# Attention on head pairs: scores on row halves and values on column halves of TensorE, denominators summed on VectorE and GpSimd

## The chip, the cores and the metric

The kernel runs on all eight cores of one Trainium2 chip, each core on two of the 16 sequences. The metric is device time in microseconds of the slowest core. Some executions fall in a slow state, in which the cores of one die show a lower granted TensorE clock. Single cores also ran at a clock of 0.98 in runs that count as fast. Where that matters I quote the median span of the *undisturbed cores*: all cores, over all runs of a kernel, with a granted clock of at least 0.984.

## The reference

One layer of an encoder: half-step SwiGLU FFN, then a mixer with two head groups, then a second FFN. The change touches the forgetting attention in the mixer (8 heads of 64):

```python
def fox_attention(q, k, v, log_f):                 # (B,S,H,64), causal
    F = cumsum(log_f)                              # decay, per head
    s = q·k * 64**-0.5 + F[t] - F[s]               # keys s <= t
    p = softmax(s)
    return p @ v
```

Width 1024, sequence 2048, FFN width 2816, two sequences per core. The kernel works on eight groups of 512 tokens per core, four per sequence. A group's mixer looks at 4, 8, 12 or 16 key tiles of 128.

## The kernel before

Each operation is recorded with what it reads and writes. A list scheduler with a price for every operation then fixes one static order per engine: mixer work has priority on TensorE, and FFN work of other token groups fills the rest. Attention went head by head, on the full 128 x 128 array. The queries of one head were padded with 64 rows of zeros, and each head's values stood beside 64 columns of ones, so that the second half of the output was the softmax denominator:

```python
V = sb("V", [128, 4, 16, 192], BF16)      # [v of even head | ones | v of odd head]
QT = sb("QT", [128, 8, T], BF16)          # one head per slot, the other 64 rows are zero
mixw = sb("mixw_t", [128, 2, 2048], BF16)
Pt = hM                                   # probabilities live in the tile of normalised inputs
...
for h in range(8):
    p, odd = h // 2, h % 2
    ob = 6 + nxt("ob", 2)
    def pv(j, r, off, W):
        lhsT = V[:, p, j, 64:192] if odd else V[:, p, j, 0:128]
        MM(banks[ob][:, off:512], [(lhsT, Pt[:, r, 0:W])], ...)
    for j in range(nj):                   # key tiles
        MM(banks[b][:, 0:W], [(KT[:, p, j * 128:(j + 1) * 128], QT[:, h, off:512])], ...)
        ACTV([... AF.Exp ...])            # ScalarE, 256 columns at a time
        if jj >= 0:
            TT(Pt[:, r, 0:128], Pt[:, r, 0:128], mask01[:], ALU.mult, ..., eng="pool")
        ...                               # pv follows two tiles later
    for q in range(4):                    # 64-row reciprocals, then one multiply
        P.op("dve", lambda e, ...: e.reciprocal(out=o_, in_=i_), ...)
    TT(cc[drow, p, :], banks[ob][drow, :], rcp[drow, :], ALU.mult, ...)
```

The FFN was scheduled in pieces of 8 matmuls (gate, up) and 11 (down).

## Time and profile before

| | before |
|---|---|
| first six runs | median 2773.08 us (2769.96 to 3190.63; the two high ones are slow) |
| profiled run, slowest core | 2773.5 us |
| TensorE busy | 2652.1 us, 96% |
| VectorE, ScalarE, GpSimd busy | 1487.3, 971.4, 260.2 us |

From the page of the kernel before, its span, part 1 (busy time and share of the span by engine, instructions) and the first line of part 4 (the chain of work that ended last):

```profile
span 2773.5 us, 42864 instructions; the slowest of 8 cores (2765.4 to 2773.5 us)
PE 2652.1 (96%) x14704; PEld 1294.4 (47%) x14704; DVE 1487.3 (54%) x2340; ACT 971.4 (35%) x2065; POOL 260.2 (9%) x479
...
PE 83%; DMA 7%; DVE 7%; issue 3%; ACT 1%; POOL 0%; DVEq 0%; POOLq 0%; SPq 0%; ACTq 0%
```

TensorE bounds the kernel. Its busy time is not its work, though. The timeline of the kernel before shows it (columns: start, duration, engine, line, operation, out<-in, form as rows*columns of the array):

```profile
1214.08 0.38 PE L310 MATMUL bank<-hM,V 128*128 128x512 bf16 x1
1214.29 0.38 PE L310 MATMUL bank<-QT,KT 128*128 128x512 bf16 x1
1214.51 0.38 PE L310 MATMUL bank<-hM,V 128*128 128x512 bf16 x1
```

Each matmul is recorded as 0.38 us, but one starts every 0.2155 us, so the records overlap. Scores and values alternate without a gap. So I count *slots*. A slot is the start-to-start time of a matmul's width: the median in this trace is 0.216 us for 512 columns, 0.163 for 384, 0.109 for 256, 0.056 for 128, and about 0.027 for the smallest. This is the formula N/2.4 + 2.5 ns of the Trainium skill, "TensorE: Matmul & The Clock Gate", Back-to-back issue gap. The section calls it the gap of isolated matmuls and gives about 131 ns (512 columns) and 81 ns (128) for a sustained stream; in this trace the stream itself has the formula's 216 and 56 ns, so I use the formula to fill a table of slots.

The groups that the change touches, kernel before (count, then busy us and mean ns, then idle time before them):

```profile
L310 PE MATMUL bank<-hM,V 128*128 128x512 bf16 x448 | 165.8, 380 | 10.6 <-DVE cc L347 6.1 <-POOL hM L347 4.3 <-issue 0.2
L310 PE MATMUL bank<-QT,KT 128*128 128x512 bf16 x448 | 157.1, 379 | 0.0
...
L347 POOL TENSOR_TENSOR hM<-hM,mask 128x128 bf16<-128x128 bf16 x256 | 109.3, 436 | 473.7 <-ACT hM L335 473.2 <-issue 0.2
```

And what TensorE waited for, kernel before (total us, times, longest):

```profile
PE bank L310 <- ACT sqF L335: 17.8, 12, 9.3
PE bank L310 <- DMA wgu<-wgus: 15.0, 6, 5.4
PE bank L310 <- DVE cc L347: 13.2, 12, 6.2
...
PE bank L310 <- DMA mixw_t<-mixws: 5.8, 6, 1.9
```

### The profile page before, as it was taken

How to read it: one execution, taken by the hardware profiler on the slowest of the kernel's cores; microseconds unless marked ns; L12 is line 12 of the kernel's file. 1: busy time of each engine (PE TensorE's matmuls, PEld its weight loads, DVE VectorE, ACT ScalarE, POOL GpSimd, SP SyncE). 2: the span in 40 equal slices, each digit the busy share in tenths (PEclk: the TensorE clock that was granted, in tenths of full speed). 3: DMA queues.
4: the chain of work that ended last, by engine and by line, in shares of the span. 5: the costliest groups of instructions: out<-in, count | busy, mean ns of one | idle time of the engine just before them, and what ended most of it. 6: DMA issues, size and time to landing. Idle time of an engine off the chain costs nothing.

```text
span 2773.5 us, 42864 instructions; the slowest of 8 cores (2765.4 to 2773.5 us)
## 1 busy us (share of the span) xinstructions
PE 2652.1 (96%) x14704; PEld 1294.4 (47%) x14704; DVE 1487.3 (54%) x2340; ACT 971.4 (35%) x2065; POOL 260.2 (9%) x479
## 2 busy tenths in 40 slices
PE   5999998899999999999999999999999999999997
PEld 2444453444454444544445444554445444544433
DVE  4334558458556535555455844567345575565433
ACT  2112313325327314177131421345112563375111
POOL 1100002022011000001000210011000110010000
PEclk9999999999999999999999999999999999999999
DMA  7866665587775644424444364433644334443453
GB/s 176 188 150 149 166 193 127 130 165 147 214 193 130 191 152 137 141 95 138 156 141 141 113 204 152 137 124 107 197 143 146 111 95 138 133 118 101 151 156 112
DMA packets 123585, 406.08 MB, mean 146 GB/s; under 512 B 14303, under 2 KB 14448, under 8 KB 122608
## 3 DMA queue, kind: packets, MB, share of 16 engines
q1 hardware_dynamic: 102688, 329.32, 36.9%
q0 software_dynamic: 20256, 73.24, 14.8%
q8 instruction: 125, 2.05, 0.3%
q10 hardware_dynamic: 432, 0.79, 0.1%
q14 instruction: 84, 0.69, 0.1%
HBM read 395.25 MB, written 59.77 MB: 164 GB/s over the span
## 4 chain that ended last, share of the span: by engine, by line
PE 83%; DMA 7%; DVE 7%; issue 3%; ACT 1%; POOL 0%; DVEq 0%; POOLq 0%; SPq 0%; ACTq 0%
PE bank L310 83%; DVE hM L780 2%; DMA wgu<-wgus 2%; DMA wgu<-wgu 1%; DMA mixw_t<-mixws 1%; DVE hF L350 1%; DVE x_sb L350 1%; DVE hM L350 1%; DVE thF L350 1%; DMA mixw_t<-mixw 1%; DMA wd<-wd 1%; DVE cc L347 0%; DVE act L347 0%; DMA y<-x_sb 0%; DMA x_sb<-x 0%
## 5 line engine op out<-in xcount | busy, mean ns | idle before, releaser
L310 PE MATMUL bank<-hF,wgu 128*128 128x512 bf16 x5280 | 1212.7, 382 | 37.6 <-DMA wgu<-wgus 15.0
L310 PEld LDWEIGHTS bank<-hF,wgu 128*128 128x128 bf16 x5280 | 508.9, 98 | 640.9 <-issue 69.9
L310 PE MATMUL bank<-act,wd 128*128 128x512 bf16 x2640 | 600.2, 379 | 4.8 <-DMA wd<-wd 3.3
L335 ACT ACTIVATE thF<-bank 128x512 f32<-128x512 f32 x352 | 210.6, 598 | 985.5 <-PE bank L310 984.6
L335 ACT ACTIVATE hM<-bank,biasT 128x256 bf16<-128x256 f32 (+1 forms) x1152 | 437.9, 471 | 144.4 <-PE bank L310 143.1
L350 DVE SCALAR_TENSOR_TENSOR thF<-thF,bank 128x512 f32<-128x512 f32 x352 | 241.4, 686 | 459.7 <-ACT thF L335 457.7
L310 PEld LDWEIGHTS bank<-act,wd 128*128 128x128 bf16 x2640 | 248.5, 98 | 287.7 <-issue 9.8
L350 DVE SCALAR_TENSOR_TENSOR x_sb<-bank,x_sb 128x512 f32<-128x512 f32 x256 | 176.7, 690 | 292.8 <-PE bank L310 291.0
L347 DVE TENSOR_TENSOR act<-bank,thF 128x512 bf16<-128x512 f32 x330 | 227.4, 689 | 170.4 <-PE bank L310 167.5
L780 DVE RECIPROCAL hM<-bank 64x128 f32<-64x128 f32 x256 | 244.4, 955 | 51.9 <-PE bank L310 36.1
L310 PE MATMUL bank<-hM,V 128*128 128x512 bf16 (+3 forms) x640 | 196.0, 348 | 10.8 <-DVE cc L347 6.1
L310 PE MATMUL bank<-hM,mixw_t 128*128 128x512 bf16 x896 | 199.8, 379 | 2.9 <-DMA mixw_t<-mixws 2.7
L310 PE MATMUL bank<-QT,KT 128*128 128x512 bf16 (+3 forms) x640 | 202.4, 347 | 0.0
L335 ACT ACTIVATE sqF<-x_sb 128x512 bf16<-128x512 f32 x176 | 108.3, 627 | 222.2 <-DVE x_sb L350 179.2
L347 POOL TENSOR_TENSOR hM<-hM,mask 128x128 bf16<-128x128 bf16 x256 | 109.3, 436 | 473.7 <-ACT hM L335 473.2
L310 PE MATMUL bank<-mixw_t,hM 128*128 128x256 bf16 x1280 | 143.8, 273 | 6.1 <-DMA mixw_t<-mixws 3.1
L310 PEld LDWEIGHTS bank<-mixw_t,hM 128*128 128x128 bf16 x1280 | 124.8, 98 | 27.1 <-issue 8.8
L310 PEld LDWEIGHTS bank<-hM,mixw_t 128*128 128x128 bf16 x896 | 86.4, 98 | 107.9 <-issue 8.1
L310 PE MATMUL bank<-cc,mixw_t 128*128 128x512 bf16 x512 | 121.2, 388 | 9.3 <-DVE cc L347 7.1
L434 POOL TENSOR_TENSOR stpM<-stvM,mhalf 128x8 f32<-128x8 f32 (+1 forms) x26 | 36.6, 1407 | 672.1 <-DVE stvM L354 672.0
L310 PEld LDWEIGHTS bank<-hM,V 128*128 128x128 bf16 x640 | 60.7, 98 | 76.8 <-issue 17.1
L434 POOL TENSOR_TENSOR stpF<-stvF,mhalf 128x4 f32<-128x4 f32 x22 | 23.5, 1069 | 708.9 <-DVE stvF L354 708.9
(114 smaller groups left out, 1545.2 us busy)
## 6 DMA issues: line engine op xcount, KB each, us to landing
wgu<-wgus SPq DMA_DIRECT2D x275, 512.0 KB, 3.8
wd<-wds SPq DMA_DIRECT2D x200, 352.0 KB, 3.2
mixw_t<-mixws SPq DMA_DIRECT2D x112, 512.0 KB, 3.9
wgu<-wgu POOLq DMA_DIRECT2D x55, 512.0 KB, 6.4
wgus<-wgu SPq DMA_DIRECT2D x44, 512.0 KB, 5.6
wd<-wd POOLq DMA_DIRECT2D x40, 352.0 KB, 5.8
wds<-wd SPq DMA_DIRECT2D x32, 352.0 KB, 4.0
x_sb<-x POOLq DMA_DIRECT2D x5, 2048.0 KB, 11.1
```

The costliest lines, as they stand in the source:

```text
L310: ins = e.matmul(out, lhsT=l, rhs=r, start=s0, stop=s1)
L335: ins = e.activation(out=out, in_=in_, func=func, **kw)
L347: return DVE(lambda e: e.tensor_tensor(out=out, in0=a, in1=b, op=op), free_n(out), reads, writes, rate, eng, level)
L350: return DVE(lambda e: e.scalar_tensor_tensor(out=out, in0=a, scalar=s, in1=b, op0=op0, op1=op1), free_n(out), reads, writes, level=level)
L434: P.op("pool", lambda e: e.tensor_tensor(out=pw[:, 0:n], in0=v[:, 0:n], in1=mhalf[:, 0:n], op=ALU.pow), [("stv", who), "mhalf"], [("stp", ...
L780: P.op("dve", lambda e, o_=rcp[drow, qs], i_=banks[ob][srow, qs]: e.reciprocal(out=o_, in_=i_), [], [PS(ob), ("hM", 6), ("hM", 7)], dur=86 ...
```

## The change

Its intent is to use both halves of the array in attention. Two heads form a pair. Their scores contract over 64 rows each, in the upper and the lower row half, at the same time. Their values fill 64 columns each, in the two column halves, at the same time. The ones columns go, so the probabilities are added up over the key tiles by VectorE (even head) and GpSimd (odd head), and four matmuls of 512 columns per pair of heads (each head's sum in two bf16 parts) with a 64-column block of ones sum over the partitions. Work comes in groups of two key tiles x two heads: two scores steps, then the values step of the group before, kept together by a new `glue` in the scheduler. (The scheduler's code and the placement of a few projections are left out.)

```diff
-        mixw = sb("mixw_t", [128, 2, 2048], BF16)
+        mixw = sb("mixw_t", [128, 3, 2048], BF16)
-        V = sb("V", [128, 4, 16, 192], BF16)
-        QT = sb("QT", [128, 8, T], BF16)
+        V = sb("V", [128, 4, 16, 128], BF16)
+        Pt = sb("Pt", [128, 8, T], BF16)
+        QT = sb("QT", [128, 4, T], BF16)
...
+        def PAIRS(items, reads, writes, switch=206.0, level=None):
+            d = switch + sum(free_n(items[i][2]) / 2.4 + 9.0 for i in range(0, len(items), 2))
...
-  [(0, 8)]                                        # FFN pieces, gate and up
+  [(0, 4), (4, 8)]
-  [(0, NC2 - 1), (NC2 - 1, NC2)] if d == 0 else [(0, NC2)]      # down
+  (0, 5), (5, NC2 - 1), (NC2 - 1, NC2)
...
+            def scores(p, js):                    # two key tiles, two heads each
+                    for e in range(2):
+                        rows = slice(64 * e, 64 * e + 64)
+                        items.append((banks[bs[2 * q + e]][:, 0:512 - off], KT[rows, p, j * 128:(j + 1) * 128],
+                                      QT[rows, p, off:512], True, True))
...
+            def probabilities(p, tiles):          # Exp on ScalarE, mask now on VectorE, then the sums
+                    for j, e, r, off, b in tiles:
+                        TT(den[:, e, off:512], den[:, e, off:512], Pt[:, r, 0:512 - off], ALU.add, [("Pt", r)], [("ga", e)],
+                           eng=("dve", "pool")[e])
+            def values(p, tiles):
+                for j, e, r, off, b in tiles:
+                    half = slice(64 * e, 64 * e + 64)
+                    items.append((banks[OB][half, off:512], V[:, p, j, half], Pt[:, r, 0:512 - off], j == 0, j == nj - 1))
+            def normalize(p):                     # split the sum into two bf16 parts, ones64 matmuls, reciprocals
...
+            for p in range(4):
+                for j in range(0, nj, 2):
+                    mm, tiles = scores(p, (j, j + 1))
+                    if last is not None:
+                        mm.glue = values(*last)
+                    if last is not None and j == 0:
+                        normalize(last[0])
+                    probabilities(p, tiles)
+                    last = (p, tiles)
```

More of the change, by code (lines that the diff above doesn't have):

```diff
@@ L27 @@
     __slots__ = ("eng", "fn", "reads", "writes", "dma_key", "stream", "idx", "deps", "waits", "signal",
-                 "count", "clock", "gidx", "dur", "lat", "prio", "start", "end", "nbytes", "users", "rate", "tset", "slack")
+                 "count", "clock", "gidx", "dur", "lat", "prio", "start", "end", "nbytes", "users", "rate", "glue", "tset", "slack")
 class Prog:
@@ L40, in op @@
         o.slack = slack
+        o.glue = None
         o.tset = tset
@@ L73, in schedule @@
             o.deps = list(deps.values())
+        for o in reversed(ops):
+            if o.glue is not None:
+                have = {id(d) for d in o.deps}
+                o.deps += [d for d in o.glue.deps if id(d) not in have and d is not o]
+                if o not in o.glue.deps:
+                    o.glue.deps.append(o)
+        for o in ops:
             for d in o.deps:
@@ L86, in schedule @@
         n_done = 0
+        placed = [False] * len(ops)
+        glued = None
         while n_done < len(ops):
@@ L89, in schedule @@
             for e in ENGINES:
+                while ready[e] and placed[ready[e][0][1]]:
+                    heapq.heappop(ready[e])
+                while soon[e] and placed[soon[e][0][1]]:
+                    heapq.heappop(soon[e])
                 if ready[e]:
@@ L97, in schedule @@
                     best = (t, e)
-            t, e = best
-            while soon[e] and soon[e][0][0] <= t:
-                g = heapq.heappop(soon[e])[1]
-                heapq.heappush(ready[e], (ops[g].prio, g))
-            g = heapq.heappop(ready[e])[1]
+            if glued is not None:
+                e, g = glued.eng, glued.gidx
+                t = free[e]
+            else:
+                t, e = best
+                while soon[e] and soon[e][0][0] <= t:
+                    g = heapq.heappop(soon[e])[1]
+                    if not placed[g]:
+                        heapq.heappush(ready[e], (ops[g].prio, g))
+                g = heapq.heappop(ready[e])[1]
             o = ops[g]
+            placed[g] = True
+            glued = o.glue
             o.start = t
@@ L275, in build_nc @@
         mhalf = sb("mhalf", [128, 16], F32)
+        ones64 = sb("ones64", [128, 64], BF16)
+        tick = sb("tick", [128, 1], F32)
         ident = sb("ident", [128, 128], BF16)
@@ L288, in build_nc @@
         wmisc = sb("wmisct", [128, 8, 40], BF16)
-        Pt = hM
-        flat = V[:].rearrange("p a b c -> p (a b c)")
-        hF2 = flat[:, 0:8 * T].rearrange("p (k t) -> p k t", k=8)
-        act2 = flat[:, 8 * T:(8 + NC2) * T].rearrange("p (k t) -> p k t", k=NC2)
+        hF2 = KT[:].rearrange("p a b -> p (a b)")[:, 0:8 * T].rearrange("p (k t) -> p k t", k=8)
+        act2 = V[:].rearrange("p a b c -> p (a b c)")[:, 0:NC2 * T].rearrange("p (k t) -> p k t", k=NC2)
         glT = pieces[96:128, :]
-        rcp = hM[:, 6:8, :].rearrange("p k t -> p (k t)").bitcast(F32)
+        rcp = sqM[:].rearrange("p r t -> p (r t)").bitcast(F32)
+        den = ga[:].rearrange("p (e t) c -> p e (t c)", e=2)
+        den_hi = lsg[:].rearrange("p (e t) c -> p e (t c)", e=2)
+        den_lo = kdec[:].rearrange("p (e t) c -> p e (t c)", e=2)
+        osum = gv[:].rearrange("p (r t) c -> p r (t c)", r=2).bitcast(F32)
         osq = hM[:, 6:8, :]
@@ L321, in MMS @@
             d = sum(max(free_n(r) / 2.4 + 3.0, 27.0) for _, _, r, _, _ in items)
+            return P.op("pe", mm_fn(items), reads, writes, dur=d, lat=280.0, level=level)
+        def PAIRS(items, reads, writes, switch=206.0, level=None):
+            d = switch + sum(free_n(items[i][2]) / 2.4 + 9.0 for i in range(0, len(items), 2))
             return P.op("pe", mm_fn(items), reads, writes, dur=d, lat=280.0, level=level)
@@ L398, in build_nc @@
         MSET(wg2a[96:128, :], 0.0, ["wg2a"], eng="dve")
-        MSET(QT[64:128, 0:8:2, :], 0.0, [("QT", p) for p in range(4)], eng="dve")
-        MSET(QT[0:64, 1:8:2, :], 0.0, [("QT", p) for p in range(4)], eng="dve")
+        MSET(ones64[:], 1.0, ["ones64"])
         MSET(pieces[0:96, :], 0.0, ["pieces"], eng="dve")
@@ L488, in ffn @@
                     bg = nxt("fb", 3)
-                    for k0, k1 in ([(0, 4), (4, 5), (5, 6), (6, 7), (7, 8)] if cnt["wgu"] == 1 else [(0, 8)]):
-                        MM(banks[bg][:], [(w4[:, 0, k, :], L.h[:, k, :]) for k in range(k0, k1)],
-                           [("wgu", wb)] + L.hk[k0:k1], [PS(bg)], start=k0 == 0, stop=k1 == 8)
                     bu = nxt("fb", 3)
-                    MM(banks[bu][:], [(w4[:, 1, k, :], L.h[:, k, :]) for k in range(8)], [("wgu", wb)] + L.hk, [PS(bu)])
+                    for g, b in ((0, bg), (1, bu)):
+                        for k0, k1 in ([(0, 4), (4, 5), (5, 6), (6, 7), (7, 8)] if cnt["wgu"] == 1 and g == 0 else [(0, 4), (4, 8)]):
+                            MM(banks[b][:], [(w4[:, g, k, :], L.h[:, k, :]) for k in range(k0, k1)],
+                               [("wgu", wb)] + L.hk[k0:k1], [PS(b)], start=k0 == 0, stop=k1 == 8)
                     r = nxt("th", 2)
@@ L506, in ffn @@
                         n += 1
-                        for c0, c1 in ([(0, NC2 - 1), (NC2 - 1, NC2)] if d == 0 else [(0, NC2)]):
+                        for c0, c1 in ((0, 5), (5, NC2 - 1), (NC2 - 1, NC2)):
                             MM(banks[b][:], [(wd[:, wb, c * 128:(c + 1) * 128], L.act[:, c, :]) for c in range(c0, c1)],
@@ L544, in ffn1_pair @@
             norm_rstd(rstdF2[:, 1], ("rstdF2", 1), 7, 0.5, "M")
-            MSET(V[:, :, :, 64:128], 1.0, [("V", p, g) for p in range(4) for g in range(4)]
+            MSET(tick[:], 0.0, [(t, p, g) for t in ("KT", "V") for p in range(4) for g in range(4)]
                  + [("hF2", k) for k in range(8)] + [("act2", c) for c in range(NC2)], eng="dve", level=0.7)
@@ L575, in chunk @@
             def chunk(i):
-                wb = nxt("mix", 2)
-                LOADW("mixw", wb, mixw[:, wb, :], mixw_d, mixw_s, i, 0, [("act", 10)] if cnt["mix"] <= 2 else ())
+                wb = nxt("mix", 3)
+                LOADW("mixw", wb, mixw[:, wb, :], mixw_d, mixw_s, i, 0, [("act", 10)] if cnt["mix"] <= 3 else ())
                 return mixw[:, wb, :].rearrange("p (k c) -> p k c", k=8), ("mixw", wb)
@@ L616, in mixer @@
             for i in range(2):
-                b = mb()
+                b = 6 + i
                 zb.append(b)
@@ L642, in mixer @@
             CP(pieces[64:72, :], fa, ["fa"], ["pieces"])
+            w3, wk = chunk(2)
+            for j in range(2):
+                proj_T(w3, wk, j * 128, lambda b, j=j: ACTV([(gq[:, j, :], banks[b][:], AF.Copy, None, 0.125)], [],
+                                                            [PS(b), ("gq", j)]))
+            for i in range(2):
+                w3, wk = chunk(6 + i)
+                for pp in range(2):
+                    p = 2 * i + pp
+                    proj_T(w3, wk, pp * 128, lambda b, p=p: ACTV([(QT[:, p, :], banks[b][:], AF.Copy, None, 0.125)], [],
+                                                                 [PS(b), ("QT", p)]))
             for i in range(2):
@@ L662, in mixer @@
                    ALU.subtract, ["fref"] + [("nFs", g) for g in range(tg + 1)], [("biasT", t)])
-            w3, wk = chunk(2)
-            for j in range(2):
-                proj_T(w3, wk, j * 128, lambda b, j=j: ACTV([(gq[:, j, :], banks[b][:], AF.Copy, None, 0.125)], [],
-                                                            [PS(b), ("gq", j)]))
-            for i in range(2):
-                w3, wk = chunk(6 + i)
-                for pp in range(2):
-                    p = 2 * i + pp
-                    proj_T(w3, wk, pp * 128, lambda b, p=p: ACTV(
-                        [(QT[64 * e:64 * e + 64, 2 * p + e, :], banks[b][64 * e:64 * e + 64, :], AF.Copy, None, 0.125)
-                         for e in range(2)], [], [PS(b), ("QT", p)]))
             for i in range(2):
@@ L683, in ev @@
                     def ev(b, i=i, t2=t2):
-                        src = banks[b][:].rearrange("p (t q e c) -> p t q e c", t=2, q=2, e=2)
-                        for q in range(2):
-                            p = 2 * i + q
-                            dst = V[:, p, 4 * tg + 2 * t2:4 * tg + 2 * t2 + 2, :].rearrange("p t (e c) -> p t e c", e=3)[:, :, 0:3:2, :]
-                            CP(dst, src[:, :, q, :, :], [], [PS(b), ("V", p, tg)])
+                        t0 = 4 * tg + 2 * t2
+                        CP(V[:, 2 * i:2 * i + 2, t0:t0 + 2, :].rearrange("p q t c -> p t q c"),
+                           banks[b][:].rearrange("p (t q c) -> p t q c", t=2, q=2), [],
+                           [PS(b), ("V", 2 * i, tg), ("V", 2 * i + 1, tg)])
                     proj_N(w3, wk, 2 * t2, ev)
@@ L747, in mixer @@
                        [("cc", 4 + h) for h in range(4)], rate=2.0)
-            for h in range(8):
-                p, odd = h // 2, h % 2
-                ob = 6 + nxt("ob", 2)
-                pend = []
-                def pv(j, r, off, W):
-                    lhsT = V[:, p, j, 64:192] if odd else V[:, p, j, 0:128]
-                    MM(banks[ob][:, off:512], [(lhsT, Pt[:, r, 0:W])], [("hM", r), ("V", p, j // 4)], [PS(ob)],
-                       start=(j == 0), stop=(j == nj - 1))
-                for j in range(nj):
-                    jj = j - 4 * tg
-                    off = jj * 128 if jj > 0 else 0
-                    W = 512 - off
-                    b = mb()
-                    r = nxt("pt", 6)
-                    MM(banks[b][:, 0:W], [(KT[:, p, j * 128:(j + 1) * 128], QT[:, h, off:512])],
-                       [("KT", p, j // 4), ("QT", p)], [PS(b)])
+            OB = 7
@@ new lines, in mixer @@
+            last = None
+            def scores(p, js):
+                r0 = 4 * nxt("pt", 2)
+                bs = [3 + i for i in range(4)]
+                mms, tiles = [], []
+                for q, j in enumerate(js):
+                    off = max(0, j - 4 * tg) * 128
+                    items = []
+                    for e in range(2):
+                        rows = slice(64 * e, 64 * e + 64)
+                        items.append((banks[bs[2 * q + e]][:, 0:512 - off], KT[rows, p, j * 128:(j + 1) * 128],
+                                      QT[rows, p, off:512], True, True))
+                        tiles.append((j, e, r0 + 2 * q + e, off, bs[2 * q + e]))
+                    mms.append(PAIRS(items, [("KT", p, j // 4), ("QT", p)], [PS(b) for b in bs[2 * q:2 * q + 2]], 103.0 - 103.0 * q))
+                mms[0].glue = mms[1]
+                return mms[1], tiles
@@ L766, in mixer @@
+            def probabilities(p, tiles):
+                for j, e, r, off, b in tiles:
+                    h = 2 * p + e
                     spans = [(max(off, t * 256), t * 256 + 256, t) for t in range(off // 256, 2)]
                     ACTV([(Pt[:, r, a - off:z - off], banks[b][:, a - off:z - off], AF.Exp, biasT[:, t, j, h:h + 1], None)
-                          for a, z, t in spans], [("biasT", t) for _, _, t in spans], [PS(b), ("hM", r)])
-                    if jj >= 0:
-                        TT(Pt[:, r, 0:128], Pt[:, r, 0:128], mask01[:], ALU.mult, ["mask01"], [("hM", r)], eng="pool")
@@ L771, in mixer @@
-                    pend.append((j, r, off, W))
-                    if len(pend) > 2:
-                        pv(*pend.pop(0))
-                for q in pend:
-                    pv(*q)
-                drow = slice(64, 128) if odd else slice(0, 64)
-                srow = slice(0, 64) if odd else slice(64, 128)
+                          for a, z, t in spans], [("biasT", t) for _, _, t in spans], [PS(b), ("Pt", r)])
+                    if e == 1 and j >= 4 * tg:
+                        TT(Pt[:, r - 1:r + 1, 0:128], Pt[:, r - 1:r + 1, 0:128],
+                           mask01[:].unsqueeze(1).broadcast_to([128, 2, 128]), ALU.mult, ["mask01"],
+                           [("Pt", r - 1), ("Pt", r)], rate=2.0)
@@ new lines, in probabilities @@
+                if tiles[0][0] == 0:
+                    for e in range(2):
+                        w = 512 - tiles[2 + e][3]
+                        if w < 512:
+                            CP(den[:, e, 0:512 - w], Pt[:, tiles[e][2], 0:512 - w], [("Pt", tiles[e][2])], [("ga", e)],
+                               eng=("dve", "pool")[e])
+                        TT(den[:, e, 512 - w:512], Pt[:, tiles[e][2], 512 - w:512], Pt[:, tiles[2 + e][2], 0:w], ALU.add,
+                           [("Pt", tiles[e][2]), ("Pt", tiles[2 + e][2])], [("ga", e)], eng=("dve", "pool")[e])
+                else:
+                    for j, e, r, off, b in tiles:
+                        TT(den[:, e, off:512], den[:, e, off:512], Pt[:, r, 0:512 - off], ALU.add, [("Pt", r)], [("ga", e)],
+                           eng=("dve", "pool")[e])
@@ new lines, in values @@
+            def values(p, tiles):
+                items = []
+                for j, e, r, off, b in tiles:
+                    half = slice(64 * e, 64 * e + 64)
+                    items.append((banks[OB][half, off:512], V[:, p, j, half], Pt[:, r, 0:512 - off], j == 0, j == nj - 1))
+                return PAIRS(items, [("Pt", t[2]) for t in tiles] + [("V", p, tiles[0][0] // 4)], [PS(OB)])
+            def normalize(p):
+                r = p % 2
+                for e in range(2):
+                    CP(den_hi[:, e, :], den[:, e, :], [("ga", e)], [("lsg", e)])
+                    TT(den_lo[:, e, :], den[:, e, :], den_hi[:, e, :], ALU.subtract, [("ga", e), ("lsg", e)], [("kdec", e)])
+                CP(osum[:, r, :], banks[OB][:], [], [PS(OB), ("gv", r, 0), ("gv", r, 1)])
+                PAIRS([(banks[OB][64 * e:64 * e + 64, :], ones64[:], d[:, e, :], d is den_hi, d is den_lo)
+                       for d in (den_hi, den_lo) for e in range(2)],
+                      ["ones64"] + [(t, e) for t in ("lsg", "kdec") for e in range(2)], [PS(OB)])
+                sq2 = [("sqM", 0), ("sqM", 1)]
+                gv2 = [("gv", r, 0), ("gv", r, 1)]
+                if p < 3:
+                    ACTV([(rcp, banks[OB][:], AF.Copy, None, None)], [], [PS(OB)] + sq2)
@@ L778, in mixer @@
                 for q in range(4):
                     qs = slice(q * 128, (q + 1) * 128)
-                    P.op("dve", lambda e, o_=rcp[drow, qs], i_=banks[ob][srow, qs]: e.reciprocal(out=o_, in_=i_), [],
-                         [PS(ob), ("hM", 6), ("hM", 7)], dur=860.0, lat=180.0)
-                TT(cc[drow, p, :], banks[ob][drow, :], rcp[drow, :], ALU.mult, [("hM", 6), ("hM", 7)], [PS(ob), ("cc", p)])
-            nb = 6 + nxt("ob", 2)
+                    src = rcp[:, qs] if p < 3 else banks[OB][:, qs]
@@ new lines, in normalize @@
+                    P.op("dve", lambda e, a=rcp[:, qs], b=src: e.reciprocal(out=a, in_=b), [],
+                         sq2 + ([PS(OB)] if p == 3 else []), dur=860.0, lat=180.0)
+                if p < 3:
+                    TT(cc[:, p, :], osum[:, r, :], rcp, ALU.mult, gv2 + sq2, [("cc", p)], eng="pool")
+                else:
+                    TT(cc[:, p, :], osum[:, r, :], rcp, ALU.mult, gv2 + sq2, [("cc", p)])
+            for p in range(4):
[7 more added lines that the diff above has]
+                    last = (p, tiles)
@@ L784, in mixer, with part @@
+            values(*last)
+            normalize(3)
+            nb = 7
             early = [4, 5, 6, 7, 0, 1, 2]
+            bs3 = [mb(), mb(), mb()]
             for i in range(4):
                 w3, wk = chunk(12 + i)
-                bs = [mb(), mb()]
-                def part(dd, cs):
+                bs = bs3[0:2] if i == 0 else bs3[2:3] + [mb()] if i == 1 else [mb(), mb()]
+                def part(dd, cs, w3=w3, wk=wk, bs=bs):
                     MM(banks[bs[dd]][:], [(w3[:, c, dd * 128:(dd + 1) * 128], cc[:, c, :]) for c in cs],
@@ L791, in part, with evac @@
                        [wk] + [("cc", c) for c in cs], [PS(bs[dd])], start=(4 in cs), stop=(3 in cs))
-                def evac(dd):
+                def evac(dd, i=i, bs=bs):
                     d = 2 * i + dd
@@ L798, in mixer @@
                 if i == 0:
+                    first, first_evac = part, evac
+                    for dd in range(2):
+                        part(dd, early)
+                elif i == 1:
                     part(0, early)
-                    part(1, early)
+                    for dd in range(2):
+                        first(dd, [3])
+                        first_evac(dd)
                     part(0, [3])
                     evac(0)
-                    part(1, [3])
+                    part(1, early + [3])
                     evac(1)
```

## The prediction

> **What bounds the kernel now.** TensorE. The page shows PE busy 96% of 2773.5 us; the chain of waits is 83% PE. Busy contains pipeline tails, so I count starts: the timeline shows dense 128x512 matmuls starting every 0.2155 us, though each is recorded as 0.38 us. Over the groups by shape (10,816 matmuls 512 wide, 1,280 projections 256 wide, the rest small), issue needs about 2606 us. Some 167 us are lost: about 41 in the first 100 us, 26 at 450-550 us (two mixers back to back), 23 at the end, the rest scattered (waits for squares 18, FFN weights 21, mixer weights 11, VectorE in attention and output projection 13). In attention ScalarE is nearly full (exponentials start every 0.365 us, gaps of 0.3 to 0.7 us), but FFN matmuls fill PE there.
>
> **What the change takes from PE.** Scores and values are 640 matmuls each, 278,528 columns each: 118 us each at the measured spacing. Scores contract 128 rows of which 64 are zeros; values spend half their columns on ones. Paired halves should take half: -118 us. The Trainium skill, "TensorE: Matmul & The Clock Gate", Part 3, says such tiles run concurrently; no trace here shows it yet.
>
> **What it adds on PE.** Denominator matmuls, 8 mixers x 4 pairs x 2 paired passes of 512: +14 us. Mode switches: the skill's "TensorEngine Tiling (Array Packing)", Key Properties, says that changing the mode drains TensorE. There are 160 groups (two scores steps, one values step, then FFN), three switches each. A recorded matmul outlives its issue slot by 0.16 us, so I estimate 0.10 to 0.16 us a switch: 48 to 77 us, about 58; plus 5 for the denominators' switches and 5 for weight loads under narrow diagonal tiles. Net -36 us, nearly all on the critical path.
>
> **Other engines.** Exponentials are unchanged. VectorE: +288 additions at about 0.69 us (+199), +110 for splitting sums and copying values, masks +25; half the reciprocals go (-122), most 64-row multiplies (-38). About 1650 us busy. GpSimd loses its masks (109 us) but gains 288 additions of 512; its 128-wide two-input operation takes 0.436 us, so I estimate 1.2 us each: about 530 us busy. "SBUF — State Buffer" (two separate sides) says VectorE with two SBUF inputs and GpSimd exclude each other; some VectorE additions should stretch, at worst delaying FFN evacuation. Per group of two key tiles: ScalarE 4.6 us, GpSimd 2.5, VectorE 3.5, so ScalarE still sets attention's pace. The next scores wait for all four exponentials: a ScalarE gap of about 1 us per group, hidden by FFN.
>
> **Smaller moves.** Own probability tiles, a third mixer-weight buffer, finer FFN pieces and the reordered output projection should return 10 to 25 us of the scattered losses. New waits (single output bank, normalisation through three engines) cost 5 to 15. Net about -10.
>
> **Prediction: 2726 us** (-1.7%), 8 in 10 between 2685 and 2768. Faster by over 2%: 0.40; within 2%: 0.56; slower by over 2%: 0.04.
>
> **What would show it.** Timeline: the second half of a scores pair starts within tens of ns of the first, the next pair 0.22 us later; gaps of 0.1 to 0.16 us at each change of mode. Groups: still 640 scores (64 rows) and 640 values (64 columns); VectorE near 1650 us, GpSimd near 530. Chain: PE still over 80%; waits on mixer weights and reciprocals shrink.
>
> **What would make it wrong.** Halves that don't overlap (about 2830); switches free (about 2670) or over 0.25 us (no gain); VectorE held up by GpSimd so that PE waits for evacuation; a gain from scattered waits above 25 us.

## The result, and the profile after

| | before | after |
|---|---|---|
| median | 2778.35 us (20 runs, slow ones among them) | 2729.72 us (10 runs, two of them slow) |
| ratio of fast runs | 1 | 0.9837 (95% interval 0.9825 to 0.9849) |
| undisturbed cores | 2766.6 to 2770.6 us (on three chips) | 2719.1 us |
| VectorE busy | 1487.3 us | 1652.6 us |
| GpSimd busy | 260.2 us | 508.6 us |

A ratio is the mean time of one kernel's fast runs over that of the other's fast runs of the same rounds, so it is not quite the ratio of the medians. Executions in which one die ran at a lower clock are left out of the means. The change takes 1.6% off the time: a small gain, clear of noise.

The page of the changed kernel, the same lines:

```profile
span 2727.5 us, 43851 instructions; the slowest of 8 cores (2711.1 to 2727.5 us)
PE 2613.5 (96%) x14832; PEld 1202.2 (44%) x14832; DVE 1652.6 (61%) x2706; ACT 960.0 (35%) x2057; POOL 508.6 (19%) x544
...
PE 83%; DMA 7%; DVE 5%; issue 3%; ACT 2%; POOL 0%; DVEq 0%; SPq 0%; POOLq 0%; ACTq 0%
```

The timeline of the changed kernel, one group of attention at 16 key tiles:

```profile
1196.01 0.61 PE L336 MATMUL bank<-QT,KT 64*128 64x512 bf16 x4
1196.51 2.30 ACT L365 ACTIVATE Pt<-bank,biasT 128x256 bf16<-128x256 f32 x6 [1.13 <-PE bank L336]
...
1196.55 0.62 PE L336 MATMUL bank<-Pt,V 128*64 128x512 bf16 x4
...
1197.10 3.63 PE L336 MATMUL bank<-hF,wgu 128*128 128x512 bf16 x16
...
1200.66 0.61 PE L336 MATMUL bank<-QT,KT 64*128 64x512 bf16 x4
```

Read it by starts. Four scores matmuls take 1196.55 - 1196.01 = 0.54 us. Two slots of 0.216 are 0.43; the other 0.11 is, by the single records, 0.093 for the change from row halves to column halves and 0.011 for a first pair that is a little slower. The second half of a pair starts 3 ns after the first. Four values matmuls take 0.55 us. Sixteen FFN matmuls take 3.56 us where 16 slots are 3.45, so the step back to row halves costs about 0.1 too. The bracket at ScalarE shows the predicted idle time of about a microsecond per group (1.13 us). A group comes every 4.65 us; the prediction gave ScalarE 4.6 us per group.

The touched groups after:

```profile
L336 PE MATMUL bank<-Pt,V 128*64 128x512 bf16 x448 | 73.0, 394 | 0.0
L336 PE MATMUL bank<-QT,KT 64*128 64x512 bf16 x448 | 70.7, 382 | 3.0 <-ACT Pt L365 2.0 <-DVE ga L377 0.5 <-DVE Pt L377 0.4
...
L377 POOL TENSOR_TENSOR ga<-ga,Pt 128x512 f32<-128x512 f32 x168 | 217.4, 1294 | 203.6 <-ACT Pt L365 150.1 <-DVE Pt L377 50.7 <-POOL ga L377 0.8
L377 DVE TENSOR_TENSOR ga<-ga,Pt 128x512 f32<-128x512 f32 x168 | 153.4, 913 | 46.8 <-ACT Pt L365 40.2 <-DVE ga L377 1.0 <-DVE x_sb L380 0.8
...
L377 DVE TENSOR_TENSOR Pt<-Pt,mask 128x256 bf16<-128x256 bf16 x128 | 52.1, 415 | 31.8 <-ACT Pt L365 31.5
```

The counts are the same, with half the busy time: overlapping halves share it. (`ga` is the tile that holds the denominators.) And TensorE's waits after:

```profile
PE bank L336 <- ACT sqF L365: 23.3, 15, 7.8
PE bank L336 <- DMA wgu<-wgus: 20.4, 8, 5.1
PE bank L336 <- DMA wgu<-wgu: 16.8, 10, 5.3
PE bank L336 <- DVE thF L380: 7.1, 13, 1.8
PE bank L336 <- DVE Pt L377: 6.6, 11, 1.6
...
PE bank L336 <- DMA mixw_t<-mixw: 5.2, 7, 1.6
```

The waits on `cc` (attention's result, 13.2 us before) and on kept mixer weights (5.8) are gone. Those on squares, FFN weights and masks have grown by about as much (one core each, the slowest).

This gives a ledger. For each core whose trace holds every matmul record, I add up the slots (a pair counts once), then the extra time at attention's changes of mode, and call the rest of the span *lost*: waits, start, end, and short stalls. All rows are means over the profiled run's complete cores (six of them, unless stated):

| kernel | span | slots | changes of mode | lost |
|---|---|---|---|---|
| before | 2769.5 | 2607.2 | 0 | 162.3 |
| changed | 2721.1 | 2506.1 | 53.9 (552 of them) | 161.1 |
| difference | -48.4 | -101.1 | +53.9 | -1.2 |

The halves take 101 us of slots away: 118 for scores and values, less 14 for the denominators, is 104, and the other 3 lie in how the ledger counts a pair. (If each pair counts as one slot by the formula, the change is -103.8, and lost time rises by 2 us and doesn't fall by 1.) The changes of mode take 54 back, 0.093 to 0.099 us each at a single change. Lost time is the same in sum, within these 3 us, with other causes.

The ledger's zero for the kernel before is for attention alone. The other head group (linear attention) has matmuls over 64 rows (a few over 17) in both kernels, and about 11 us for their changes of mode stand under lost time in both. So the trace from which the prediction was made already showed what it had to estimate. Kernel before, core 7:

```profile
374.70 0.71 PE L310 MATMUL bank<-mixw_t,hM 128*128 128x256 bf16 x5
375.34 0.40 PE L310 MATMUL bank<-gv,kdec 64*128 64x256 bf16 x4
375.67 0.60 PE L310 MATMUL bank<-act,wd 128*128 128x512 bf16 x2
```

Five slots of 0.109 us from 374.70 end at 375.25, and the next step starts 0.1 us later: by the single records each such change costs 0.096 us on the way in and 0.093 on the way out. Four matmuls, two on one row half and then two on the other, take 0.33 us, which is two slots and a change, not four slots: the single records start in pairs 7 ns apart. Where two of the same half stand alone, they start 0.12 us apart.

### The profile page after: what moved, and what is told of

Same layout as the page of the kernel before. It is cut to its first block, busy times and chain, and to the rows that moved or that the text cites. A ratio compares the mean times of both kernels' runs of the same rounds, so it can differ in the third digit from the quotient of the medians.

```text
span 2727.5 us, 43851 instructions; the slowest of 8 cores (2711.1 to 2727.5 us)
## 1 busy us (share of the span) xinstructions
PE 2613.5 (96%) x14832; PEld 1202.2 (44%) x14832; DVE 1652.6 (61%) x2706; ACT 960.0 (35%) x2057; POOL 508.6 (19%) x544
## 4 chain that ended last, share of the span: by engine, by line
PE 83%; DMA 7%; DVE 5%; issue 3%; ACT 2%; POOL 0%; DVEq 0%; SPq 0%; POOLq 0%; ACTq 0%
PE bank L336 83%; DMA wgu<-wgu 3%; DMA wgu<-wgus 2%; DMA mixw_t<-mixw 1%; DVE x_sb L380 1%; DVE hF L380 1%; ACT Pt L365 1%; DMA mixws<-mixw_t 1%; DVE Pt L377 0%; DVE thF L380 0%; DVE sqM L840 0%; DVE ga L377 0%; DMA x_sb<-x 0%; DMA y<-x_sb 0%; DVE hM L380 0%
## 5 line engine op out<-in xcount | busy, mean ns | idle before, releaser
L336 PEld LDWEIGHTS bank<-hF,wgu 128*128 128x128 bf16 x5280 | 497.3, 98 | 685.3 <-issue 147.6
L336 PE MATMUL bank<-act,wd 128*128 128x512 bf16 x2640 | 608.9, 379 | 1.0 <-DVE x_sb L380 1.0
L365 ACT ACTIVATE Pt<-bank,biasT 128x256 bf16<-128x256 f32 (+1 forms) x1152 | 430.0, 477 | 153.7 <-PE bank L336 151.4
L336 PEld LDWEIGHTS bank<-act,wd 128*128 128x128 bf16 x2640 | 242.9, 97 | 283.4 <-issue 22.6
L377 POOL TENSOR_TENSOR ga<-ga,Pt 128x512 f32<-128x512 f32 (+3 forms) x256 | 284.6, 1112 | 264.5 <-ACT Pt L365 150.1
L377 DVE TENSOR_TENSOR ga<-ga,Pt 128x512 f32<-128x512 f32 (+3 forms) x256 | 201.2, 786 | 52.9 <-ACT Pt L365 40.2
L336 PE MATMUL bank<-mixw_t,hM 128*128 128x256 bf16 x1280 | 141.7, 273 | 4.0 <-DMA mixw_t<-mixw 4.0
L336 PE MATMUL bank<-QT,KT 64*128 64x512 bf16 (+3 forms) x640 | 86.9, 349 | 9.2 <-DVE Pt L377 6.6
L840 DVE RECIPROCAL sqM<-sqM 128x128 f32<-128x128 f32 x96 | 90.7, 944 | 7.3 <-ACT sqM L365 5.9
L380 DVE SCALAR_TENSOR_TENSOR hF<-x_sb,gT,rstdF 128x512 bf16<-128x512 f32 x120 | 89.6, 796 | 2.5 <-ACT rstdF L365 2.0
```

Source lines behind the costliest of these rows:

```text
L336: ins = e.matmul(out, lhsT=l, rhs=r, start=s0, stop=s1)
L365: ins = e.activation(out=out, in_=in_, func=func, **kw)
L377: return DVE(lambda e: e.tensor_tensor(out=out, in0=a, in1=b, op=op), free_n(out), reads, writes, rate, eng, level)
L380: return DVE(lambda e: e.scalar_tensor_tensor(out=out, in0=a, scalar=s, in1=b, op0=op0, op1=op1), free_n(out), reads, writes, level=level)
L840: P.op("dve", lambda e, a=rcp[:, qs], b=src: e.reciprocal(out=a, in_=b), [], sq2 + ([PS(OB)] if p == 3 else []), dur=860.0, lat=180.0)
```

## The experiments

Theory: the gain is the halves' overlap on the critical path, less the changes of mode; the side changes and the new waits cancel. Rivals: the gain comes from the side changes (buffers, finer pieces), or ScalarE's pace decides in attention and TensorE's work there is off the critical path, or the sums on two engines hold the change back. Ratios below are to the kernel before, three rounds each. The twelve kernels ran in three batches, each on one chip.

### Scores pairs forced onto one half

```diff
-                        rows = slice(64 * e, 64 * e + 64)
+                        rows = slice(0, 64)
```

> The changed kernel with one edit: both scores matmuls of a pair read rows 0 to 63, so that they must share one half of the array (wrong result on purpose; the order of instructions on every engine is unchanged). Theory (the gain is the overlap of the halves, on the critical path): each pair takes two slots, 58.8 us more issue time over the 320 pairs, so about 2730 + 59 = 2789 us, ratio to before about 1.005; TensorE's time from the start of a full scores step to the start of the values step grows from 0.54 to about 0.97 us. Rival 1 (the gain comes from the buffers, the finer pieces and the order): stays within 10 us of 2730. Rival 2 (ScalarE's pace decides in attention): also stays, because the extra 0.43 us a group is less than ScalarE's group of 4.6 us.

The result was wrong. The order on every engine is that of the changed kernel. The ratio was 1.0023 (0.9957 to 1.0089) on a chip where single cores were disturbed; the undisturbed cores stand at 2762.6 us against 2719.1, +43.5 us. The timeline of this kernel shows a full scores step taking 0.96 us:

```profile
1211.37 1.03 PE L336 MATMUL bank<-QT,KT 64*128 64x512 bf16 x4
1212.33 0.62 PE L336 MATMUL bank<-Pt,V 128*64 128x512 bf16 x4
```

Ledger: slots 2563.5 (+57.4), changes of mode 53.2, lost 146.6 (-14.5). So the overlap is real, two matmuls on the same half take two slots, and both rivals, which expected no change, fall. This is shown for the scores; no run forces the values onto one half, and there the timeline (four in 0.55 us) and the ledger stand alone. Of 57 us of extra TensorE work only about 43 reached the time: a busier TensorE covers some waits that it would otherwise have stood in. The expectation of +59 took slots for time; the measured rise was a quarter smaller.

### Values ordered half by half

```diff
-                return PAIRS(items, ...)
+                o = PAIRS(items, ...)
+                o.fn = mm_fn(items[0::2] + items[1::2])     # lower, lower, upper, upper
+                return o
```

> The changed kernel with the four values matmuls of a group issued lower, lower, upper, upper half instead of lower, upper, lower, upper (right result, same order otherwise). Theory: tiles overlap only with a neighbour in the order on another half, so a group takes three slots instead of two: about +29 us, 2759 us, ratio about 0.9945; a full values step goes from 0.55 to about 0.77 us. Rival (overlap doesn't depend on the order, or the halves are off the critical path): no change, 2730 us.

No change: undisturbed cores 2721.2 us against 2719.1, ratio 0.9877 (0.9801 to 0.9952; some runs had disturbed cores). My theory of the hardware was wrong here, and the four matmuls of the kernel before that are shown under the ledger, also issued half by half, had already spoken against it. At a diagonal group, the widths are issued 512, 384, 512, 384, and the records start 512 and 512 within 6 ns, then 384 and 384 after 240 ns. The third matmul started before the second: here one half did not hold up the other.

### Five changes of mode for each group

(The edit also divides the scheduler's charge for a change of mode, so that the total stays.)

```diff
+                    if q == 0 and between is not None:
+                        mms.append(values(between[0], between[1][0:2]))
...
-                    mm, tiles = scores(p, (j, j + 1))
+                    mm, tiles = scores(p, (j, j + 1), last)
                     if last is not None:
-                        mm.glue = values(*last)
+                        mm.glue = values(last[0], last[1][2:4])
```

> The changed kernel with each group's steps taken in turn: scores, half of the values, scores, half of the values, so five changes of mode a group instead of three (right result; the scheduler is charged the same total, so that its order stays). Theory (a change of mode costs about 0.094 us on TensorE and nothing hides it): 159 groups x 2 x 0.094 = +30 us, about 2760 us, ratio about 0.995; the sum of the extra at changes of mode in the trace goes from 54 to about 84 us. Rival (switches hide behind waits): less than 8 us.

The undisturbed cores stand at 2747.7 us, +28.6; ratio 0.997 (0.9897 to 1.0043). The timeline of this kernel:

```profile
1208.44 0.39 PE L336 MATMUL bank<-QT,KT 64*128 64x512 bf16 x2
1208.76 0.41 PE L336 MATMUL bank<-Pt,V 128*64 128x512 bf16 x2
1209.10 0.39 PE L336 MATMUL bank<-QT,KT 64*128 64x512 bf16 x2
1209.42 0.41 PE L336 MATMUL bank<-Pt,V 128*64 128x512 bf16 x2
1209.76 3.63 PE L336 MATMUL bank<-hF,wgu 128*128 128x512 bf16 x16
```

Each pair of one slot now takes 0.32 to 0.34 us. Ledger: 856 changes cost 92.2 us, slots 2505.8, lost 150.4. So 304 more changes added 38 us on TensorE, of which about 29 reached the time. The expected +30 us was met because two misses cancelled: the changes cost more than expected, and a quarter of the cost did not reach the time. A change after a step of one slot costs more (0.10 to 0.12 us) than one after a longer step (0.09 to 0.10).

### Three side changes undone together, and one by one

Together: two mixer-weight buffers, coarse FFN pieces, probability tiles in the `hM` tile.

```diff
-        mixw = sb("mixw_t", [128, 3, 2048], BF16)
-        Pt = sb("Pt", [128, 8, T], BF16)
+        mixw = sb("mixw_t", [128, 2, 2048], BF16)
+        Pt = hM
-  [(0, 4), (4, 8)]   and   (0, 5), (5, NC2 - 1), (NC2 - 1, NC2)
+  [(0, 8)]           and   (0, 10), (10, 11) for the first output, else (0, 11)
```

> The changed kernel without three of its side changes: two mixer-weight buffers instead of three, FFN pieces of 8 and 11 matmuls as before, and the probability tiles in the hM tile again. The prediction's term says that they returned 10 to 25 us: 2740 to 2755 us. The ledger of the two traces says that the lost time is the same in both kernels (about 145 and 150 us), so if the side changes pay at all, it is only because new waits cost as much. Rival 1 (they carry the whole gain): about 2774 us, ratio 1.0. If they are worth nothing: 2730 us.

Ratio 0.9979 (0.9922 to 1.0036). Its cores ran at a granted clock of 0.98 throughout, so the mean span of the six complete cores in the profiled run is used: 2745.9 us, with 187.5 us lost (+26 against the change). A look at the gaps shows where: TensorE waited up to 9.5 us for the result of attention near 690 us, and stood idle in steps of 2 to 7 us near 2565 to 2610 us, at the end of the last mixer, where no FFN work was left to fill. These gaps go with the low clock, which is the kernel's own and not the chip's: the other three kernels of the batch had cores at 0.99 on that chip, this one had none above 0.982 in four runs. On core 4 the granted clock was 0.66 from 690 to 720 us and 0.70 from 2563 to 2625; the changed kernel (core 1) had 1.00 from 690 to 720 and from 2500 to 2625. So part of the 26 us is matmuls at a lower clock near the gaps. Then each alone:

> The changed kernel with two mixer-weight buffers instead of three, all else kept. The run with three side changes undone lost about 28 us of undisturbed cores' time against the changed kernel (2747 against 2719 us). Theory: the largest part of that is the coarse FFN pieces; this one costs under 8 us (waits for mixer weights were 11 us in the kernel before, 5 to 7 in the changed one): undisturbed cores at 2719 to 2727 us. Rival: it is the buffer; then about 2740.

Two buffers alone: undisturbed cores 2718.6 us, ratio 0.9811 (0.9787 to 0.9835), but only two of six runs were fast. Worth nothing by itself.

> The changed kernel with FFN pieces of 8 and 11 matmuls as before, all else kept. Theory: coarse pieces make each group of attention late by up to half a piece, ScalarE idles longer, attention lasts longer, and FFN work to fill the last mixer runs out: +12 to +25 us, undisturbed cores at 2731 to 2744 us. Rival (pieces don't matter): 2719 to 2723 us.

Coarse pieces alone: 2729.3 us, +10, a little less than expected; ratio 0.9857 (0.984 to 0.9874). Lost time 170.2 us.

> The changed kernel with the probability tiles in the hM tile again, all else kept. Theory: the next mixer's normalisation and the GLA squares wait for the last values of attention, +4 to +12 us, undisturbed cores at 2723 to 2731 us. Rival: this is the side change that counts, +20 or more.

Shared probability tiles alone: 2717.7 us, ratio 0.9823 (0.9806 to 0.984). Worth nothing by itself, less than expected.

> The kernel before with only the finer FFN pieces of the change (the other two side changes do not fit in its memory). If finer pieces pay by themselves, without the halves, 2755 to 2765 us, ratio 0.994 to 0.998. If they pay only where groups of four tiles must be issued at once (the changed kernel), no change: ratio 0.999 to 1.001.

Finer pieces in the kernel before: ratio 1.0091 (0.9993 to 1.0189), undisturbed cores 2775.9 us against 2766.6: no gain, perhaps a loss. So the finer pieces pay only beside the new groups. Together the three are worth about 25 us in the changed kernel, but singly 0, 10 and 0; every edit also makes the scheduler choose another order, and which pair of them acts together was not tested. Nor was the reordered output projection, the fourth move that the prediction counted.

### The changed kernel again, and the sums on VectorE alone

> The changed kernel itself, as a reference on this chip: about 2729 us, undisturbed cores at 2719 us.

2730.92 us (median of four runs, one slow), ratio 0.9821 (0.9801 to 0.984), undisturbed cores 2723.1 us: the reference for this chip.

```diff
-                           eng=("dve", "pool")[e])
+                           eng="dve")
```

(in all three places where the denominators are summed)

> The changed kernel with all sums of probabilities on VectorE, none on GpSimd. Theory (the two engines shut each other out while both read two operands): a full addition on VectorE falls from 0.913 to about 0.69 us although there are twice as many; VectorE's busy time is 2 x 285 additions at about 0.65 us, in all about 1800 us. In time: VectorE is still under the 4.65 us that ScalarE sets for a group (4 x 0.69 + 1.4 for FFN = 4.2 us), so within 10 us of the change, 2719 to 2729 us on undisturbed cores. Rival (the change is held up by GpSimd, prediction's third doubt): faster than the change by 10 us or more. Rival (VectorE then sets the pace): slower by over 20 us.

2708.7 us, ratio 0.975 (0.9735 to 0.9766), undisturbed cores 2701.7 us. This beats both kernels: 0.975 / 0.9821 = 0.993, 0.7% faster than the change in the same rounds. The rival that I had given little weight won. The page, the sums and TensorE's waits of this kernel:

```profile
span 2705.7 us, 43407 instructions; the slowest of 8 cores (2693.2 to 2705.7 us)
PE 2606.4 (96%) x14832; PEld 1199.8 (44%) x14832; DVE 1713.6 (63%) x3002; ACT 958.6 (35%) x2057; POOL 182.0 (7%) x248
```

```profile
L377 DVE TENSOR_TENSOR ga<-ga,Pt 128x512 f32<-128x512 f32 x336 | 233.1, 725 | 24.3 <-ACT Pt L365 19.3 <-DVE thF L380 0.5 <-DVE Pt L377 0.5
L377 DVE TENSOR_TENSOR Pt<-Pt,mask 128x256 bf16<-128x256 bf16 x128 | 37.9, 310 | 16.0 <-ACT Pt L365 15.6
```

```profile
PE bank L336 <- ACT sqF L365: 17.1, 7, 10.4
...
PE bank L336 <- DVE thF L380: 5.7, 12, 1.1
...
PE bank L336 <- DVE Pt L377: 1.6, 5, 0.7
```

Twice as many additions raise VectorE's busy time by only 61 us (1652.6 to 1713.6), because every one got shorter. In the changed kernel a full addition on VectorE takes 0.69 us when no addition or product on GpSimd overlaps it (52 cases) and 1.15 us when one is running at its start (83 cases). A mask takes 0.28 us against 0.69, a normalisation of `hF` 0.74 against 1.40. The FFN step on `thF`, with one operand in PSUM, takes 0.68 us either way. That is what the Trainium skill, "SBUF — State Buffer" (two separate sides), says: a VectorE instruction with two SBUF inputs and a GpSimd one that reads SBUF exclude each other for the whole instruction. The trace agrees closely: of the 83 additions that began while GpSimd ran, at least eight in ten end 0.546 to 0.558 us after that GpSimd operation ends.

Ledger: slots 2505.9, changes of mode 53.3, lost 141.7 us against 159.1 for the changed kernel on this chip. So 17 of the 18 us between the two profiled runs' complete cores (21 us between the undisturbed cores) come from lost time. The waits on masks (6.2 to 1.6 us on the slowest cores) and on squares (24.9 to 17.1) fall; those on FFN weights do not. What stays open: the static order differs too, since the scheduler charges the two engines differently. The stretching of single instructions is shown; that it alone makes the 18 us is argued.

### Values once for two groups

(Cut.)

```diff
-                        mm.glue = values(*last)
+                    if len(last) == 2:
+                        mm.glue = values(last[0][0], last[0][1] + last[1][1])
```

> The changed kernel with the values step done once for two groups (eight matmuls), so that half of the groups need two changes of mode and not three (right result). Theory (0.094 us a change, nothing hides it): 80 changes fewer, -7.5 us: undisturbed cores at about 2711 us. Rival: with only eight probability tiles the exponentials of every other group wait for the longer values step, and the gain is lost: 2719 us or more.

Undisturbed cores 2717.7 us against 2723.1, ratio 0.9806 (0.9791 to 0.9822) against 0.9821 (0.9801 to 0.984). The changes of mode fell as expected, from 552 to 457 and from 54.0 to 45.1 us, but lost time was 163.4 against 159.1 us. The gain of about 5 us is within the intervals: inconclusive.

> As the one before, with twelve probability tiles, for which the third mixer-weight buffer is given up (alone it was worth nothing): the wait of the exponentials is gone. Theory: 2709 to 2713 us on undisturbed cores, the fastest of all. Rival: as the change, 2719 us.

Slower: ratio 0.9882 (0.9863 to 0.9902), undisturbed cores 2742.3 us. Changes of mode again cost 45.8 us, but lost time was 185.3. Waits for kept mixer weights came back (12.9 us on the slowest core) and those on `thF` rose to 20.1 us. The theory was wrong to call the third buffer free because it was worth nothing in another order. This run does not separate the two edits.

## Why the prediction was right

- **Time.** Predicted 2726 us (2685 to 2768, within 2% the likeliest), measured 2729.72 us, ratio 0.9837.
- **Halves overlap.** Predicted -118 + 14 = -104 us of slots; the ledger has -101.1. Shown for the scores by the same-half run: +57 us of slots, +43 us of time. The prediction rested the overlap on the skill; the trace of the kernel before had it too.
- **Changes of mode.** Predicted 0.10 to 0.16 us each, 63 us with the denominators'. Measured 0.093 to 0.099 us each, 53.9 us in all, just under the lower end of the estimate. The skill says that a change of mode drains TensorE ("TensorEngine Tiling (Array Packing)", Key Properties); the trace shows time lost at every change, and the five-changes run shows its price. The estimate came from the length of a record, where the kernel before had 114 such changes at 0.091 to 0.096 us to read it from.
- **Narrow weight loads: the size right by luck.** Predicted 5 us under narrow diagonal tiles; stalls of 20 to 80 ns beyond the slot sum to 7.2 us after and 2.3 before. But 4.6 of the 7.2 are 24 ns in each of 192 steps on column halves (values and denominators), between its two pairs, whatever the width. Why is not shown.
- **Other engines.** VectorE about 1650 us, measured 1652.6; GpSimd about 530, measured 508.6. That VectorE's total fits is luck in part: the 288 additions took 231 us by their records where 199 were predicted, because they were held up. ScalarE keeps the pace: attention at 16 key tiles lasts about 157 us where it was 132 to 140, and FFN fills it.
- **Smaller moves: the mis-sized term.** The prediction said "Net about -10": 10 to 25 us returned by the side changes, 5 to 15 taken by new waits. Lost time fell by 1.2 us in the ledger (or rose by 2, if a pair counts as one slot), and it holds the 5 us of stalls that the prediction charged apart; so the smaller moves brought 3 to 6 us. The three side changes are worth about 25 us in the changed kernel, at the top of the estimate, but the new waits take most of it back. Sums on two engines that shut each other out are the largest piece found: with VectorE alone 18 us came back, though the order changed too. The prediction named this as a risk and did not charge it.
- **Two errors cancelled.** The changes of mode were about 9 us too dear in the sum, the slots and the smaller moves together about 7 us too good. The total was nearer than its parts.

## What to carry to other kernels

In this kernel, pairing half-filled matmuls paid the saved slots minus 0.09 to 0.10 us for every change of mode, so count the changes per group before counting the gain. Look first whether the trace that you have already holds such a change: here it did. In the two runs that added TensorE work, about three quarters of it reached the time (43 of 57 us, 29 of 38). Giving half of an elementwise load to GpSimd is not free help: where both engines read two SBUF operands, VectorE alone was faster here with only 4% more busy time. Judge side changes in the kernel that they serve: finer FFN pieces were worth 10 us beside the new groups and nothing without them.

## What the Trainium skill lacked or had wrong

- "TensorE: Matmul & The Clock Gate", Part 3 ("MATMULs are pc-monotone in start AND end — strict FIFO, no reordering"): not so for starts here. Issued with widths 512, 384, 512, 384 on the halves lower, lower, upper, upper, the records start 512, 512 (6 ns apart), then 384, 384 (at 240 and 246 ns). About ends the trace says nothing, since they are modelled.
- "TensorEngine Tiling (Array Packing)", Key Properties, says that changing the mode drains TensorE and gives no price: 0.093 to 0.099 us a change after steps of two slots or more, 0.10 to 0.12 us after steps of one slot.
- "TensorE: Matmul & The Clock Gate", Part 3, has measured speedups for packs of three and more tiles, none for a stream of pairs: here two pairs of 512 columns take two slots of 0.216 us and 0.01 to 0.02 us more.
- "SBUF — State Buffer" (two separate sides) has the exclusion of VectorE and GpSimd, but no time for an elementwise operation that is held up: a VectorE addition of 512 columns takes 0.69 us alone and 1.15 us on average when a GpSimd operation is running at its start, most ending 0.55 us after that operation.
